# Top-k of the second mask in four pieces beside the first mask's scores, and mLSTM's q and k chunks set apart by v and the gates

## The chip, the cores and the metric

The kernel runs on one core of a Trainium2 chip. The engines named here are PE (TensorE, the matmul array; PEld is its weight load), DVE (VectorE), ACT (ScalarE), POOL (GpSimd) and SP (SyncE, which issues most DMAs). The metric is the device time of one execution in microseconds (us), as the median of several runs: 2522.85 us before, of 2522.05, 2522.85 and 2522.98.

## The reference

The program is a chain of blocks over 256 tokens of width 1024, all in fp32: two layers, each a mixer with three parallel branches and a SwiGLU feed-forward; then retention, a feed-forward, a short convolution, and a mixture of eight experts with a final norm. The change touches the mixer alone, which runs twice. Cut to what matters, it computes:

```python
def _layer(x, li, ...):
    z = rms(x, norm_mix_g) @ w_in
    (m_qk, m_v, m_o, m_if, s_q, s_ckv, i_q, i_k, i_w, d_q, d_k, d_v, g_pre) = split(z)
    m_qk = silu(causal_conv(m_qk, conv_w, conv_b))          # 4 taps, 1024 channels
    y_a = sigmoid(m_o) * rms(mlstm(mq, mk, m_v, m_if))      # 4 heads of 128
    y_b = dsa(rope(rms(s_q)), sk, sv, iq, ik, i_w)          # 8 heads of 64
    y_c = rms(diff_attn(rope(rms(d_q)), rope(rms(d_k)), d_v, lam))   # 4 heads, 2 x 64
    gates = sigmoid(g_pre + b_gate)                         # 3 x 1024
    merged = (gates[0] * (y_a @ w_branch[0]) + gates[1] * (y_b @ w_branch[1])
              + gates[2] * (y_c @ w_branch[2]))
    return x + merged @ w_out                               # then the feed-forward

def dsa(q, k, v, qi, ki, wi):        # for each query:
    score = sum over the 4 index heads of wi * relu(qi . ki), causal
    idx = top_k(score, 64)           # the 64 best keys of the 256
    return softmax(q . k[idx] / 8) @ v[idx]

def diff_attn(q, k, v, lam):
    p = softmax(causal(q . k / 8))   # for both halves of a head
    return (p[half 0] - lam * p[half 1]) @ v
```

## The kernel before

**Large matmuls.** An fp32 matmul is made of three: weights and activations are split into a high part and a rest, and high times high, rest times high and high times rest are added in PSUM (L224 to L226 in `gemm`; L256 to L258 in `gemmT`, which makes the transposed result). Weights come raw from memory by SP's queue into 4 buffers of 1 MB; for each 128x1024 piece ACT makes the high part (`hi`, L217) and DVE subtracts (`lo`, L218), each into one of 3 buffers. PE can work on such a chunk only as fast as both of them supply it, and runs at most 3 pieces behind. Results gather in 4 PSUM banks called `acc`; all small matmuls and transposes of the branches use 4 other banks called `mm`. A chunk of 512 output columns is 48 matmuls of 512 columns; its last matmul is followed by an evacuation on DVE or ACT that frees its two banks.

**Branches.** In `mixer` three generators hold the branches' small steps: `s` (the sparse attention, `dsa`), `f` (the differential attention, `diff`) and `m` (`mlstm`). Each `yield` ends a step. The string ORDER says in which order steps and chunks are written: a letter `s`, `f` or `m` takes the next step of that generator (nothing if it has ended); `dq`, `dk`, `dv`, `mv`, `o0`, `o1`, `q0` to `q3` (mLSTM's q and k, 256 columns each, by `gemmT`) and `g0` to `g5` (gates, 512 columns each) are chunks of the input projection; `b0`, `b1`, `c0`, `c1`, `a0`, `a1` are chunks of a branch's output projection, and the first of each drains that branch's generator. A scheduler then fixes each engine's queue in advance; the order in which things are written is their priority there. Every engine runs its own queue in order, so a matmul that waits holds all matmuls behind it.

**The sparse attention's steps.** After the scores of the index heads, the top-k of each of the two 128-query blocks (t = 0 and 1) is 8 rounds of MAX8 and MATCH_REPLACE8 on DVE (L588, L589), over 128 keys for t = 0 and 256 for t = 1; L592 to L594 make the mask from it. Then for each t four head pairs follow: scores on PE (L609), minus row maximum and mask on DVE (L547, `masked`), exponentials on ACT (L614), a transpose through PE (L539) and a copy by ACT (L541, `pT_of`), and the product with v on PE (L619).

**The differential attention's steps.** For the q and k rows: squares on ACT, sums, rope and norm on DVE (L460 to L462, L473, L481), the power for the norm on POOL (L192), and transposes on PE (L299). For each t, two head pairs: scores on PE (L675), `masked` (L547), exponentials with sums on ACT (L681), reciprocals (L686, L687), the scaling on ACT (L689) and the difference on DVE (L690), then a transpose (L539), its copy (L541) and the product with dv (L696). At a t's end ACT copies the row block out (`orow`, L700) and squares it four times (L470), POOL makes the power, DVE scales (L703); after both t, L274 transposes `orow`.

**Evacuations near the change.** A q chunk's result is scaled into `zp` (L740) and convolved (L746, three L748), with a tanh on ACT (L749) and L750. A gate chunk's is scaled and biased on DVE (L845; the bias row `bg` is loaded by SP for each chunk, L843) and goes through a tanh on ACT (L846). A line above 600 of the kernel before stands about 9 lines further down in the changed kernel: L539 and L547 are the same, L675 becomes L684, L696 becomes L705, L690 becomes L699, L845 becomes L854, L588 becomes L587.

Of the kernel before, what the change touches and what calls it, by code (L numbers as in the profile page):

```python
# [10 lines left out]
F32 = mybir.dt.float32  # L11
# [8 lines left out]
P = 128  # L20
# [6 lines left out]
NE = 8  # L27
BIG = 1e30
FILL = float(np.float32(1.5e38))
ORDER = ('dq s o0 s dv mg dk s o1 s s s s q0 s q1 s mh q2 q3 s s s s g3 s s g2 mv '  # L30
         'b0 f f f f f b1 f f f g4 f f g5 f m m m m g0 m m g1 c0 m c1 a0 a1')
WARM = 12
PRI1 = 200
NR1 = 3
# [15 lines left out]
TAKEN = float(np.float32(-3.3e38))  # L50
# [63 lines left out]
class Net:  # L114
# [305 lines left out]
    def mixer(self, li):  # L420
        nc, tc, I, sp = self.nc, self.tc, self.I, self.sp
        X = self.X
        with ExitStack() as es:
            zp_ = es.enter_context(tc.tile_pool(name="z4", bufs=18))
            mp = es.enter_context(tc.tile_pool(name="mix", bufs=1))
            tp = es.enter_context(tc.tile_pool(name="tmp", bufs=2))
            w2_ = es.enter_context(tc.tile_pool(name="w2", bufs=10))

            def z4(name, shape=(P, 2, 512), dt=F32):
                return zp_.tile(list(shape), dt, tag="z4", name=name)  # L430

            def w2(name, shape=(P, 512)):
                return w2_.tile(list(shape), F32, tag="w2", name=name)
# [92 lines left out]
            def qk_rows(src, which, dstT):  # L526
                rows = [w2("qkr") for _ in range(2)]
                for t in range(2):
                    normrope(src[:, t], which, rows[t], t)
                return lambda: self.plain_T(lambda t: rows[t], 4, dstT)  # L530

            def pT_of(prow, npair, t):

                pt = w2("pT")
                ps = self.mm_tile()
                k = 0
                for j in range(npair):
                    for s in range(t + 1):
                        nc.tensor.transpose(ps[:, k * P:(k + 1) * P], prow[:, j, s * P:(s + 1) * P], self.idt)  # L539
                        k += 1  # L540
                nc.scalar.copy(pt[:, :k * P], ps[:, :k * P])  # L541
                return pt[:, :k * P].rearrange("p (j s q) -> p j s q", j=npair, s=t + 1)

            def masked(dst, psv, m, nk, nm):

                for j in range(2):
                    nc.vector.tensor_tensor_reduce(dst[:, j, :nk], psv[:, j], m, -1.0, BIG, ALU.add, ALU.min, nm[:, j:j + 1])  # L547
# [3 lines left out]
            def new_yT():  # L551
                return z4("yTh", (P, 4, S), F32R), z4("yTl", (P, 4, S), F32R)

            def dsa():

                smask, scs = [None, None], [None, None]
                for t in range(2):
                    nk = P * (t + 1)
                    sc = tp.tile([P, 256], F32, tag="sc", name="sc")
                    nc.vector.memset(sc[:, :nk], 0.0)  # L560
                    for hp in range(2):
                        ps = self.mm_tile()
                        b = slice(hp * 64, hp * 64 + 64)
                        for j in range(2):
                            nc.tensor.matmul(ps[:, j * S:j * S + nk], iT[b, j, t * P:(t + 1) * P], iT[b, 2, :nk],
                                             start=True, stop=True)
                        rl = w2("rl", (P, 2, 256))
                        nc.scalar.activation(rl[:, :, :nk], ps.rearrange("p (j s) -> p j s", j=2)[:, :, :nk], AF.Relu)
                        for j in range(2):
                            h = j * 2 + hp  # L570
                            nc.vector.scalar_tensor_tensor(sc[:, :nk], rl[:, j, :nk], wi[:, t, h:h + 1], sc[:, :nk],
                                                           op0=ALU.mult, op1=ALU.add)
                    dsl = slice(t * P, (t + 1) * P)
                    nc.vector.tensor_tensor(sc[:, dsl], sc[:, dsl], self.cap, op=ALU.min)
                    scs[t] = sc
                sqT, skT = z4("sqT", (P, 4, S)), z4("skT", (P, 4, S))
                turn = qk_rows(zs, 0, sqT)
                yield
                turn()
                turn = qk_rows(skr, 1, skT)  # L580
                yield
                turn()
                for t in range(2):
                    nk = P * (t + 1)
                    sc, dsl = scs[t], slice(t * P, (t + 1) * P)
                    for i in range(8):
                        m8 = tp.tile([P, 8], F32, tag="m8", name="m8")  # L587
                        nc.vector.max(m8, sc[:, :nk])  # L588
                        nc.vector.match_replace(sc[:, :nk], m8, sc[:, :nk], TAKEN)  # L589
                    m = mp.tile([P, 256], BF16, name="smask", tag="smask%d" % t)  # L590
                    if t:
                        nc.vector.tensor_scalar(sc[:, :P], sc[:, :P], TAKEN, None, op0=ALU.is_equal)  # L592
                    nc.vector.scalar_tensor_tensor(sc[:, dsl], sc[:, dsl], TAKEN, self.lo01, op0=ALU.is_equal, op1=ALU.mult)
                    nc.vector.tensor_scalar(m[:, :nk], sc[:, :nk], -1.0, BIG, op0=ALU.add, op1=ALU.mult)  # L594
                    smask[t] = m
                    yield
                yb = z4("yb")
                for t in range(2):
                    nk = P * (t + 1)
                    po = self.mm_tile()  # L600
                    den = tp.tile([P, 8], F32, tag="den", name="den")
                    for q in range(4):
                        heads = [(q // 2) * 4 + (q % 2) + 2 * j for j in range(2)]
                        b = slice((q % 2) * 64, (q % 2) * 64 + 64)
                        ps = self.mm_tile()
                        psv = ps.rearrange("p (j s) -> p j s", j=2)[:, :, :nk]
                        for j in range(2):
                            hp = heads[j] // 2
                            nc.tensor.matmul(psv[:, j], sqT[b, hp, t * P:(t + 1) * P], skT[b, hp, :nk], start=True, stop=True)  # L609
                        nm = tp.tile([P, 2], F32, tag="nm", name="nm")  # L610
                        pr = w2("pr", (P, 2, 256))
                        masked(pr, psv, smask[t][:, :nk], nk, nm)
                        for j in range(2):
                            nc.scalar.activation(pr[:, j, :nk], pr[:, j, :nk], AF.Exp, bias=nm[:, j:j + 1], scale=-1.0,  # L614
                                                 accum_out=den[:, heads[j]:heads[j] + 1])
                        pt = pT_of(pr, 2, t)
                        for j, h in enumerate(heads):
                            for s in range(t + 1):
                                nc.tensor.matmul(po[:, h * 64:(h + 1) * 64], pt[:, j, s], sv[:, s, h * 64:(h + 1) * 64],  # L619
                                                 start=s == 0, stop=s == t)  # L620
                        if q < 3:
                            yield
                    rd = tp.tile([P, 8], F32, tag="rd", name="rd")
                    nc.vector.reciprocal(rd, den)
                    nc.vector.tensor_mul(yb[:, t].rearrange("p (h d) -> p h d", d=64), po.rearrange("p (h d) -> p h d", d=64),
                                         rd[:, :, None].to_broadcast([P, 8, 64]))
                    yield
                yT["b"] = new_yT()
                self.split_T(lambda t: yb[:, t], 4, *yT["b"])


            dq, dk, dv = {}, {}, {}
# [218 lines left out]
            def branch(key, b, c0):  # L851
                def ev(t, c0, n, ps):
# [6 lines left out]

            mqk_chunk = lambda c0: (lambda: self.gemmT(xs, 8, W, [c0], ev_qk))  # L860
            gens = {"s": dsa(), "f": diff(), "m": mlstm()}
            work = {"dq": chunk(3148, 512, ev_into(dq, "dq")), "dk": chunk(3660, 512, ev_into(dk, "dk")),
                    "dv": chunk(4172, 512, ev_into(dv, "dv")), "mv": chunk(1024, 512, ev_mv),
# [5 lines left out]
            for key, gen, b in (("b", "s", 1), ("c", "f", 2), ("a", "m", 0)):  # L869
                for hf in range(2):  # L870
# [4 lines left out]
                    work["%s%d" % (key, hf)] = br  # L875
            for w in ORDER.split():
                if w in gens:
# [479 lines left out]
```

## Time and profile before

| what | value |
|---|---|
| median of 3 runs | 2522.85 us |
| profiled execution | 2522.33 us |
| its span | 2520.2 us |
| its granted PE clock, mean | 0.994 of full |
| the two mixers | about 5 to 270 us and 480 to 750 us of the span |

All times of rows are microseconds from the start of the span of that one execution, unless a column says otherwise. The time outside the span is 2.1 us. An engine's busy time counts what overlaps once; the 512-column matmuls of the chunks are pipelined, so that one lasts 0.39 us in its row while the next starts 0.23 us after it. The clock column is what the throttle granted to PE: 1.00 is 2.4 GHz, 0.50 is 1.2 GHz.

### The profile page before, as it was taken

What the parts mean: (1) busy time and instruction counts of PE and PEld (TensorE: products, weight loads), DVE (VectorE), ACT (ScalarE), POOL (GpSimd) and SP (SyncE); (2) the same over time, 40 slices, a digit from 0 to 9 for tenths busy, and PEclk for the clock granted to TensorE, in tenths of its full rate; (3) what the DMA queues carried; (4) which work ended last, traced back from release to release, by engine and by line L of the source; (5) the groups of instructions that cost most, each with busy time, mean ns of one, the idle gap of its engine ahead of it and who ended that gap; (6) DMA issues with size and microseconds to landing.
All of it is one profiled execution on the core that took longest, in us unless ns stands there. A gap on an engine that the chain in (4) does not pass through costs nothing. (4 is left out here: it accounts for less than half of the span.)

```text
span 2520.2 us, 32185 instructions
## 1 busy us (share of the span) xinstructions
PE 2483.6 (99%) x12113; PEld 2050.6 (81%) x12113; DVE 1888.0 (75%) x2533; ACT 1569.0 (62%) x2127; POOL 71.3 (3%) x47
## 2 busy tenths in 40 slices
PE   9999999999999999999999999999999999999997
PEld 8877888888788888878888988888887888788886
DVE  6987755578785457445555869999988898889887
ACT  6556544565655445545444448878777777777776
POOL 0110000020100000000000000000000000000000
PEclk9999999999999999999999999999999999999999
DMA  6544555464545556546555847999999999999993
GB/s 236 174 156 151 175 184 180 159 197 138 171 158 177 191 172 204 170 161 238 187 191 189 291 160 264 349 355 349 361 360 340 347 349 368 345 347 348 374 349 143
DMA packets 325139, 614.78 MB, mean 244 GB/s; under 512 B 10984, under 2 KB 44016, under 8 KB 324848
## 3 DMA queue, kind: packets, MB, share of 16 engines
q1 hardware_dynamic: 324192, 610.97, 70.3%
q8 instruction: 97, 1.59, 0.2%
q0 software_dynamic: 352, 1.06, 0.1%
q10 hardware_dynamic: 432, 0.62, 0.1%
q14 instruction: 66, 0.54, 0.1%
HBM read 611.55 MB, written 1.06 MB: 243 GB/s over the span
## 5 line engine op out<-in xcount | busy, mean ns | idle before, releaser
L218 DVE TENSOR_TENSOR lo<-raw,hi 128x1024 fp32r<-128x1024 f32 (+1 forms) x1156 | 1376.9, 1215 | 545.6 <-ACT hi L217 528.6
L217 ACT CAST hi<-raw 128x1024 fp32r<-128x1024 f32 (+1 forms) x1156 | 1188.3, 1047 | 703.3 <-PE acc L226 353.5
L225 PE MATMUL mm<-lo,gh 128*128 128x512 f32 x896 | 353.2, 394 | 1.1
L224 PE MATMUL mm<-hi,gh 128*128 128x512 f32 x896 | 349.4, 390 | 2.6 <-ACT ST L1163 2.5
L226 PE MATMUL mm<-hi,gl 128*128 128x512 f32 x896 | 348.9, 390 | 0.0
L226 PE MATMUL acc<-hi,hTl 128*128 128x512 f32 x736 | 290.4, 395 | 0.0
L225 PE MATMUL acc<-lo,hTh 128*128 128x512 f32 x736 | 289.6, 394 | 0.0
L224 PE MATMUL acc<-hi,hTh 128*128 128x512 f32 x736 | 289.0, 393 | 0.0
L224 PE MATMUL acc<-hi,xTh 128*128 128x512 f32 (+3 forms) x672 | 254.8, 382 | 2.6 <-ACT hi L217 2.2
L225 PE MATMUL acc<-lo,xTh 128*128 128x512 f32 (+3 forms) x672 | 252.7, 377 | 1.3 <-DVE lo L218 1.2
L226 PE MATMUL acc<-hi,xTl 128*128 128x512 f32 (+3 forms) x672 | 250.8, 375 | 0.0
L224 PE MATMUL mm<-hi,xTh 128*128 128x512 f32 (+1 forms) x608 | 230.3, 379 | 0.0
L226 PE MATMUL mm<-hi,xTl 128*128 128x512 f32 (+1 forms) x608 | 229.8, 378 | 0.0
L225 PE MATMUL mm<-lo,xTh 128*128 128x512 f32 (+1 forms) x608 | 229.8, 378 | 0.0
L225 PEld LDWEIGHTS mm<-lo,gh 128*128 128x128 f32 x896 | 168.1, 188 | 50.9 <-DVE lo L218 17.1
L224 PEld LDWEIGHTS mm<-hi,gh 128*128 128x128 f32 x896 | 168.2, 188 | 38.7 <-ACT ST L1163 2.9
L226 PEld LDWEIGHTS mm<-hi,gl 128*128 128x128 f32 x896 | 168.2, 188 | 33.8
L224 PEld LDWEIGHTS acc<-hi,hTh 128*128 128x128 f32 x736 | 138.3, 188 | 28.1
L225 PEld LDWEIGHTS acc<-lo,hTh 128*128 128x128 f32 x736 | 138.3, 188 | 27.5
L226 PEld LDWEIGHTS acc<-hi,hTl 128*128 128x128 f32 x736 | 138.4, 188 | 26.6
L224 PEld LDWEIGHTS acc<-hi,xTh 128*128 128x128 f32 x672 | 127.6, 191 | 26.9 <-ACT hi L217 2.6
L225 PEld LDWEIGHTS acc<-lo,xTh 128*128 128x128 f32 x672 | 127.6, 190 | 24.6 <-DVE lo L218 3.6
(364 smaller groups left out, 3032.4 us busy)
## 6 DMA issues: line engine op xcount, KB each, us to landing
raw<-in_moe_w_up SPq DMA_DIRECT2D x112, 1024.0 KB, 6.5
raw<-in_moe_w_down SPq DMA_DIRECT2D x112, 1024.0 KB, 6.5
raw<-in_moe_w_gate SPq DMA_DIRECT2D x112, 1024.0 KB, 6.8
raw<-in_w_in SPq DMA_DIRECT2D x52, 1024.0 KB, 5.1
raw<-in_w_gate_up SPq DMA_DIRECT2D x40, 1024.0 KB, 5.1
raw<-in_ret_w_in SPq DMA_DIRECT2D x24, 1024.0 KB, 5.0
raw<-in_w_down SPq DMA_DIRECT2D x20, 1024.0 KB, 5.0
raw<-in_ffn_w_gate SPq DMA_DIRECT2D x14, 1024.0 KB, 5.1
```

The source lines that it names most:

```text
L217: nc.scalar.copy(hi[:, :m], r)
L218: nc.vector.tensor_sub(lo[:, :m], r, hi[:, :m].bitcast(F32))
L224: mm(ps, xh, wh, start=first, stop=False)
L225: mm(ps, xh, wl, start=False, stop=False)
L226: mm(ps, xl, wh, start=False, stop=last)
```

## The change

The second mask's eight rounds are no longer a step of their own. Two rounds are written behind each of the four head-pair steps of t = 0, and the mask behind the last; so `s` has one step fewer before the scores. In ORDER the chunks q0 to q3 are put apart: mv, g3 and g2 move from behind the sparse attention to between them, q3 moves to directly before b0, and the steps `s` are spread anew. At the end one `m` step (mLSTM) goes ahead of the `f` that stood behind g5 (before: `g5 f m m m m g0`, now: `g5 m f m m m g0`).

```diff
@@ -27,8 +27,8 @@
 NE = 8
 BIG = 1e30
 FILL = float(np.float32(1.5e38))
-ORDER = ('dq s o0 s dv mg dk s o1 s s s s q0 s q1 s mh q2 q3 s s s s g3 s s g2 mv '
-         'b0 f f f f f b1 f f f g4 f f g5 f m m m m g0 m m g1 c0 m c1 a0 a1')
+ORDER = ('dq s o0 s dv mg dk s o1 s q0 s s mv s q1 s mh g3 s q2 s g2 s s q3 '
+         'b0 f f f f f b1 f f f g4 f f g5 m f m m m g0 m m g1 c0 m c1 a0 a1')
 WARM = 12
 PRI1 = 200
 NR1 = 3
@@ -580,20 +580,25 @@
                 turn = qk_rows(skr, 1, skT)
                 yield
                 turn()
-                for t in range(2):
+
+                def rounds(t, n):
+                    for i in range(n):
+                        m8 = tp.tile([P, 8], F32, tag="m8", name="m8")
+                        nc.vector.max(m8, scs[t][:, :P * (t + 1)])
+                        nc.vector.match_replace(scs[t][:, :P * (t + 1)], m8, scs[t][:, :P * (t + 1)], TAKEN)
+
+                def chosen(t):
                     nk = P * (t + 1)
                     sc, dsl = scs[t], slice(t * P, (t + 1) * P)
-                    for i in range(8):
-                        m8 = tp.tile([P, 8], F32, tag="m8", name="m8")
-                        nc.vector.max(m8, sc[:, :nk])
-                        nc.vector.match_replace(sc[:, :nk], m8, sc[:, :nk], TAKEN)
                     m = mp.tile([P, 256], BF16, name="smask", tag="smask%d" % t)
                     if t:
                         nc.vector.tensor_scalar(sc[:, :P], sc[:, :P], TAKEN, None, op0=ALU.is_equal)
                     nc.vector.scalar_tensor_tensor(sc[:, dsl], sc[:, dsl], TAKEN, self.lo01, op0=ALU.is_equal, op1=ALU.mult)
                     nc.vector.tensor_scalar(m[:, :nk], sc[:, :nk], -1.0, BIG, op0=ALU.add, op1=ALU.mult)
                     smask[t] = m
-                    yield
+                rounds(0, 8)
+                chosen(0)
+                yield
                 yb = z4("yb")
                 for t in range(2):
                     nk = P * (t + 1)
@@ -618,6 +623,10 @@
                             for s in range(t + 1):
                                 nc.tensor.matmul(po[:, h * 64:(h + 1) * 64], pt[:, j, s], sv[:, s, h * 64:(h + 1) * 64],
                                                  start=s == 0, stop=s == t)
+                        if t == 0:
+                            rounds(1, 2)
+                            if q == 3:
+                                chosen(1)
                         if q < 3:
                             yield
                     rd = tp.tile([P, 8], F32, tag="rd", name="rd")
```

How the queues change is shown at three places of the first layer; the second layer has the same pieces. First PE's queue in the middle of the differential attention, in the kernel before: L539 transposes the probabilities (`ar`) of t = 0's second head pair, L696 is their product with dv, L675 (256 columns) the scores of t = 1's first pair, and `acc<-` rows are matmuls of a gate chunk.

```order
L224 MATMUL acc<-hi,xTh 128x512
L539 MATMUL mm<-ct,ar 128x128 x2
L675 MATMUL mm<-dkT,dqT 128x256 x3
L696 MATMUL mm<-dv,pT 128x128 x2
L675 MATMUL mm<-dkT,dqT 128x256
L225 MATMUL acc<-lo,xTh 128x512
L226 MATMUL acc<-hi,xTl 128x512
L224 MATMUL acc<-hi,xTh 128x512
L225 MATMUL acc<-lo,xTh 128x512
```

Behind these rows 34 more matmuls of gate chunks follow before the next small step. In the changed kernel the same steps (L684 and L705 are L675 and L696 of before) stand so on PE; the row after the last shown is the first matmul of g0:

```order
L539 MATMUL mm<-ct,ar 128x128 x2
L705 MATMUL mm<-dv,pT 128x128 x2
L684 MATMUL mm<-dkT,dqT 128x128 x4
L539 MATMUL mm<-ct,ar 128x128
L684 MATMUL mm<-dkT,dqT 128x256
L539 MATMUL mm<-ct,ar 128x128
L684 MATMUL mm<-dkT,dqT 128x256 x2
L705 MATMUL mm<-dv,pT 128x128 x2
L684 MATMUL mm<-dkT,dqT 128x256
L539 MATMUL mm<-ct,ar 128x128 x4
L705 MATMUL mm<-dv,pT 128x128 x4
L684 MATMUL mm<-dkT,dqT 128x256 x4
```

Here L539 and L705 first finish t = 0's first pair; then come that block's second pair (L684 x4, two L539, L705) and t = 1's first pair with the scores of its second, and no chunk matmul stands among these 12 rows. Between the scores of a pair and its transposes there stand 19 chunk matmuls for t = 0's first pair, none for its second, none for t = 1's first, and 25 for the last; before there were 19, 36 and 31 for the last three.

The second place is DVE's queue where the first mask is made (`smask`) and the first scores of t = 0 arrive (L547 writes `pr`); MAX and MATCH_REPLACE over 128x256 are rounds of the second mask. Before:

```order
L588 MAX m_1009<-sc 128x8
L593 SCALAR_TENSOR_TENSOR sc<-sc,ct 128x128
L589 MATCH_REPLACE sc<-m_1009,sc 128x256
L594 TENSOR_SCALAR smask<-sc 128x128
L218 TENSOR_TENSOR lo<-raw,hi 128x1024
L588 MAX m_1012<-sc 128x8
L547 ISA pr,nm<-mm,smask 128x128
L547 ISA nm 128x1
L589 MATCH_REPLACE sc<-m_1012,sc 128x256
L547 ISA pr,nm<-mm,smask 128x128
L547 ISA nm 128x1
```

And in the changed kernel, where L587 and L588 are the rounds and L596 and L597 the mask:

```order
L587 MAX m_1028<-sc 128x8
L596 SCALAR_TENSOR_TENSOR sc<-sc,ct 128x128
L588 MATCH_REPLACE sc<-m_1028,sc 128x256
L597 TENSOR_SCALAR smask<-sc 128x128
L218 TENSOR_TENSOR lo<-raw,hi 128x1024
L547 ISA pr,nm<-mm,smask 128x128
L547 ISA nm 128x1
L547 ISA pr,nm<-mm,smask 128x128
L547 ISA nm 128x1
L587 MAX m_1031<-sc 128x8
L588 MATCH_REPLACE sc<-m_1031,sc 128x256
```

One MAX of the second mask stands behind the first two L547 instead of ahead of them, and the rounds follow in pairs behind each step.

The third place is DVE's queue from the rows that make the sparse attention's result ready for b0 (`yTl`, L281) on, where the differential attention's q rows are normed and roped (L460 to L462). Before:

```order
L281 TENSOR_TENSOR yTl<-mm,yTh 128x512 x2
L845 SCALAR_TENSOR_TENSOR gate<-acc,xrs,bg 128x512
L218 TENSOR_TENSOR lo<-raw,hi 128x1024
L845 SCALAR_TENSOR_TENSOR gate<-acc,xrs,bg 128x512
L190 TENSOR_SCALAR rsqv<-ss 128x8
L460 TENSOR_TENSOR rp<-dq,tabs 128x512
L218 TENSOR_TENSOR lo<-raw,hi 128x1024
L845 SCALAR_TENSOR_TENSOR gate<-acc,xrs,bg 128x512 x2
L218 TENSOR_TENSOR lo<-raw,hi 128x1024
L461 TENSOR_TENSOR qkr<-dq,tabs 128x512
L460 TENSOR_TENSOR rp<-dq,tabs 128x512
```

In the changed kernel (L749, L755, L757 and L759 are q3's evacuation and convolution, L864 the merge of branch b, L854 would be a gate's):

```order
L281 TENSOR_TENSOR yTl<-mm,yTh 128x512 x2
L749 TENSOR_TENSOR zp<-acc,bc 128x256 x2
L218 TENSOR_TENSOR lo<-raw,hi 128x1024
L755 TENSOR_SCALAR cv<-zp,gc 128x256 x2
L757 SCALAR_TENSOR_TENSOR cv<-zp,gc,cv 128x256 x3
L218 TENSOR_TENSOR lo<-raw,hi 128x1024
L757 SCALAR_TENSOR_TENSOR cv<-zp,gc,cv 128x256 x2
L864 SCALAR_TENSOR_TENSOR gate<-gate,acc 128x512
L218 TENSOR_TENSOR lo<-raw,hi 128x1024
L759 SCALAR_TENSOR_TENSOR mqk<-zp,cv 128x256
L757 SCALAR_TENSOR_TENSOR cv<-zp,gc,cv 128x256
```

The rows for a gate's evacuation are gone from here, and q3's convolution and branch b's merge stand there instead; the first row of the differential attention's norm (L190) follows two rows below the last one shown.

## Rows read from the trace of the kernel before

**Rows 1.** Page, busy time of each engine.

```profile
PE 2483.6 (99%) x12113; PEld 2050.6 (81%) x12113; DVE 1888.0 (75%) x2533; ACT 1569.0 (62%) x2127; POOL 71.3 (3%) x47
```

**Rows 2.** Waits of PE: line, releaser, us in total, times, longest.

```profile
PE mm L539 <- ACT pr L614: 3.4, 3, 2.1
...
PE mm L274 <- DVE orow L703: 1.8, 2, 0.9
PE mm L299 <- DVE qkr L481: 1.4, 2, 0.7
...
PE mm L539 <- DVE ar L690: 0.6, 2, 0.3
```

**Rows 3.** Timeline of PE (start, duration): second head pair of t = 0.

```profile
194.99 0.72 PE L675 MATMUL mm<-dkT,dqT 64*128 64x128 f32 x8
195.64 0.50 PE L224 MATMUL acc<-hi,xTh 128*128 128x512 f32 x1
...
200.33 0.50 PE L539 MATMUL mm<-ct,ar 128*128 128x128 f32 x2
200.76 1.13 PE L675 MATMUL mm<-dkT,dqT 64*128 64x256 f32 x6
```

**Rows 4.** Timeline of ACT and DVE in that stretch and behind it.

```profile
197.63 1.04 ACT L217 CAST hi<-raw 128x1024 fp32r<-128x1024 f32 x1
197.75 0.18 DVE L686 RECIPROCAL dden<-dden 128x4 f32<-128x4 f32 x1 [1.09 <-ACT dp L681]
...
198.57 0.69 ACT L689 ACTIVATE dp<-dp,dden 128x128 f32<-128x128 f32 x2
...
199.84 0.61 DVE L690 SCALAR_TENSOR_TENSOR ar<-dp,dden 128x128 f32<-128x128 f32 x2
...
201.02 0.36 ACT L541 COPY pT<-mm 128x256 f32<-128x256 f32 x1
202.56 0.58 ACT L700 COPY orow<-mm 128x512 f32<-128x512 f32 x1 [1.18 <-PE mm L696]
203.18 0.31 ACT L470 ACTIVATE sq<-orow 128x128 f32<-128x128 f32 x1
...
204.37 0.49 ACT L681 ACTIVATE dp<-dp,nm 128x256 f32<-128x256 f32 x1
```

**Rows 5.** Windows: stretch, us, busy of each engine (x), PEclk, DMA, GB/s.

```profile
99.60:103.00 3.40, 3.40 (x19) 3.40 (x18) 3.11 (x9) 1.30 (x4) 0.00 (x0) 0.50 0.63 214
...
228.00:230.00 2.00, 1.09 (x8) 0.70 (x7) 1.34 (x3) 1.17 (x2) 0.63 (x1) 1.00 0.00 0
```

**Rows 6.** Timeline of DVE and POOL: norm and rope of the differential attention.

```profile
172.98 4.28 POOL L192 TENSOR_TENSOR rsq<-rsqv,nhalf 128x8 f32<-128x8 f32 x1 [1.06 <-DVE rsqv L190]
...
179.21 1.22 DVE L218 TENSOR_TENSOR lo<-raw,hi 128x1024 fp32r<-128x1024 f32 x1
180.34 0.16 DVE L190 TENSOR_SCALAR rsqv<-ss 128x8 f32<-128x8 f32 x1
180.42 0.68 DVE L460 TENSOR_TENSOR rp<-dk,tabs 128x512 f32<-128x512 f32 x1
181.02 0.68 DVE L461 TENSOR_TENSOR qkr<-dk,tabs 128x512 f32<-128x512 f32 x1
...
183.23 0.69 DVE L481 TENSOR_TENSOR qkr<-qkr,rsq 128x512 f32<-128x512 f32 x1 [0.80 <-POOL rsq L192]
...
204.74 1.01 POOL L192 TENSOR_TENSOR rsq<-rsqv,nhalf 128x4 f32<-128x4 f32 x1 [21.55 <-DVE rsqv L190]
```

**Rows 7.** Groups of DVE by line: min/median/max ns, first and last start.

```profile
L748 DVE SCALAR_TENSOR_TENSOR cv<-zp,gc,cv x48: 462/476/482, 108.5 to 617.3; 128x256 f32<-128x256 f32 x48
...
L845 DVE SCALAR_TENSOR_TENSOR gate<-acc,xrs,bg x24: 730/743/751, 156.5 to 723.5; 128x512 f32<-128x512 f32 x24
```

**Rows 8.** Timeline of DVE: second mask's round ahead of the first scores.

```profile
98.05 0.42 DVE L588 MAX8 m<-sc 128x8 f32<-128x256 f32 x1
98.39 0.27 DVE L547 CUSTOM_DVE_ANT_0 pr<-mm,smask 128x128 f32<-128x128 f32 x1
```

## The prediction

> **What bounds the kernel now.** I read the page's busy times first: PE is busy 2483.6 us of the 2520.2 us span [rows 1], so only 36.6 us of it are without a matmul, and DVE (75%) and ACT (62%) have room on the average. The kernel is bound by PE, and the change neither adds nor takes a matmul. It can win only some of the 36.6 us, but it can lose any amount, by opening holes in PE's queue. Second, PE's waits [rows 2]: those in the two mixers that the change touches are small (L539 on the sparse attention's `pr` 3.4 us, L274 on `orow` 1.8, L299 on `qkr` 1.4, L539 on `ar` 0.6, all over both layers). Third, the timeline around the differential attention, to see why they are small: a head pair's chain (scores, mask, exponentials, difference, transposes) takes from 194.99 to 200.33, 5.34 us, and 19 chunk matmuls run meanwhile [rows 3]; they fill 4.69 us, 0.25 us each with the change-over. The cover hides the chain, so its length costs only the 0.3 us per layer at `ar`. Last, the order of PE's instructions in the changed kernel: this cover is what moved.
>
> **The dense stretch (both layers).** ORDER now spends g2, g3 and mv on the sparse attention, and g4 and g5 are used up when the differential attention's first pair has its scores transposed. The twelve rows shown above follow each other on PE with no chunk matmul, and since PE's queue runs in order, g0's matmuls behind them can't start early, even with their weights there. I walk through it, in us from the first pair's scores, whose cover of 19 matmuls stands as before:
> - 5.3: the first pair's transposes, as before. Their product L705 needs ACT's copy, which now stands behind two casts in ACT's queue; before, the 1.06 us of score matmuls between transposes and product covered it [rows 3]. A copy 0.36 and part of the casts (1.04 each) [rows 4], which began while the matmuls still ran: 0.9 idle.
> - The second pair's scores, 0.65 as at 194.99 to 195.64, and then its chain bare. In the trace it took 5.34, but a cast (1.04 at 197.63) and a `lo` subtraction stood in it on ACT and DVE. Without them, the reciprocals from 197.75 take 0.5, then one half of L689 (0.35) and L690, and the transposes follow L690's start by 0.5 [rows 4, 3]: about 199.1. That makes 4.1, of which the scores are 0.65: 3.5 idle. The scores of t = 1's first pair run between its two transposes and after.
> - The product waits for its copy (0.36 and the hand-over): 0.5 idle.
> - t = 1's first pair. ACT copies `orow` (0.62 with the hand-over), squares it four times (203.18 to 204.37: 1.19), and only then makes the four exponentials (4 x 0.49 = 1.98) [rows 4]; reciprocals 0.5, L698 0.45 for 256 columns, L699 0.45 follow. 5.2, against 0.3 of scores on PE with some hand-overs: 5.1 idle.
> - The product of t = 1's first pair waits for a copy of 512 columns: 0.75 idle.
> In sum 10.75 idle per layer, against about 0.5 in the same steps before (0.3 at `ar` [rows 2], some tenths at the products): +10.3 per layer, **+20.6**. Nothing gives it back: DVE and ACT fill three pieces of weights ahead while PE idles, but afterwards PE works off its chunks at its own speed. Bounds per layer: 5.1 if only the long wait stands and the others hide in hand-overs, 13 if two more copies and casts get in the way; over both layers +10 to +26. I take the walk, since each link has a row.
>
> **The clock behind it.** After the 2.1 us wait at L539 [rows 2] PE ran the 3.4 us from 99.60 at a granted clock of 0.50 (1.2 GHz); a wait of 0.9 us at 229 left it at 1.00 [rows 5]. The stretch has waits of 3.5 and 5.1 us in each layer. If 3.4 us behind each stretch, and the small matmuls in it, go at half speed, it is 1.7 + 0.3 per layer: **+4.0**, from 0 to +6.8 (twice that behind each stretch). The Trainium skill ("TensorE: Matmul & The Clock Gate", section "HAM oscillation — how this bites in real kernels") says that waits between bursts of matmuls put the array back to half rate and that the next burst starts there; the row at 99.60 agrees. By it the sum is as I give it, without it 4.0 less.
>
> **The differential attention's rows.** q3 is now directly ahead of b0, so its convolution (12 instructions of 0.40 to 0.48 [rows 7]) and tanh lie on DVE and ACT where q and k are normed and roped; two gate evacuations (0.74 each) left that place. From b0's first evacuations to the last transposes DVE has by the changed order 9 `lo` at 1.13 (179.21 to 180.34 [rows 6]), 12 of the convolution at 0.40 apart, 4 of branch b's merge and 19 rows of 512 columns at 0.60 apart (180.42 to 181.02 [rows 6]): 10.2 + 4.8 + 13.8 = 28.8, with the small ones 29.1. PE has 120 chunk matmuls at 0.23 and small ones there: 29.0. Before there was slack, and the wait at L299 was 0.7 a layer [rows 2]. With DVE as full as PE, the powers on POOL between L190 and L481 (2.9 us from 180.34 to 183.23, of which 0.80 was idle [rows 6]) show. I take 1.5 more per layer: **+3.0**, from -1.8 (both waits and the hand-overs go) to +7 (each power's wait shows). A power took 4.28 us beside a busy DVE and 1.01 beside an idle one [rows 6]. The Trainium skill ("GPSIMD Engine Reference", section "8. Key points") says that POOL shares its way to SBUF with DVE; the two rows agree. In the dense stretch the power of `orow` isn't on the path that I walked, but behind it; at 4.28 there it would add up to 3.3 per layer, and the sum would be about 2554.
>
> **What is won.** The transposes of `orow` had 11 chunk matmuls behind t = 1's last product and waited 0.9 per layer [rows 2]; now 29 stand there: **-1.8** (0 to -1.8). In the sparse attention one MAX stood ahead of the first two L547 (98.05 to 98.39: 0.34 [rows 8]) and now stands behind them; with the later waits at `pr` (one of 0.4 a layer) that makes **-1.4** (0 to -5: all of L539's 3.4 and the half clock behind it). The 16 instructions of the second mask's rounds are the same, and run beside scores which DVE finishes early enough.
>
> **The rest.** The last head pairs of the sparse attention lie beside g2, whose two evacuations on DVE (0.74 each [rows 7]) and tanh on ACT get between softmax and transposes: **+1.0** (0 to +1.5). The `m` step written ahead of `f` changes DVE's and ACT's queue by a few short rows that PE doesn't wait for: 0, up to +0.5 if the decay weights come ahead of a mask. The bias rows come by SP as before.
>
> **Sum.** 20.6 + 4.0 + 3.0 - 1.8 - 1.4 + 1.0 = +25.4. On the profiled execution's 2522.33 this gives 2547.7; the median of the runs before is 0.5 above that execution, so 2548.
>
> **Rivals.**
> - B, not slower: PE's stretch is no stretch. Each chain finishes while PE does the step in front of it, because ACT and DVE, without casts to make, run ahead of PE. Then the stretch adds at most 1.6 per layer (the copies), L299's waits go (-1.8) and the gains stand (-1.8, -1.4): 2522.85 + 3.2 - 5.0 = 2521 at most, 2518 with no copy to wait for. It decides if a bare chain is below about 1.5 us. Against it: the chain's links lie one behind the other in rows 3 and 4 and add up to over 4 us.
> - C, heavier: the clock stays at 0.50 through the stretch and longer, and norm and rope come late by the whole power wait. 2548 + 2.8 (clock to its bound) + 4 (to its bound of 7) + 3 (casts in the chains) = 2558. For it: two holes of over 3 us so close together; against: PE was back at full clock 3.4 us after the wait at 97 [rows 5].
> - D, lighter: only the wait behind `orow` and the squares stands (5.1 per layer), and the clock doesn't fall: 2522.85 + 10.2 + 3.0 - 3.2 + 1.0 = 2534. For it: ACT and DVE have little else to do in the stretch, so hand-overs may be shorter.
>
> **How the numbers follow.** My forecast has 0.74, with its own range from 2537 to 2558; C 0.13, D 0.08, B 0.05. The range from 2533 to 2560 takes in D and C and leaves out B and what lies beyond the bounds. About 0.2% (5 us) is what a measurement of this kernel can tell from no change. B is split between faster and no change; a D that is lighter still adds nothing there: faster 0.02, same 0.03, slower 0.95.
>
> **What would show it right or wrong.** The profile's waits of PE should have new rows for L539 on `ar` (L699) of about 8 to 9 us per layer, in two waits of 3 to 4 and about 5 us, and L705 on the copy (L541) of about 2 per layer. A window of the stretch should show PE busy under half of some 15 us, and the clock at 0.50 behind it. L274 on `orow` should be gone, L299 on `qkr` should have grown to 3 to 5 in all, and L539 on `pr` should be around 2 to 3. Wrong would be: chunk matmuls in the stretch, or chains below 2 us there.

## The result, and the profile after

The changed kernel takes 2554.45 us (median of 4 runs, 2552.35 to 2557.0), against 2522.45 for the kernel before on the same chip: a ratio of 1.0131, with a 95% interval from 1.0119 to 1.0143. It is slower by 32 us; 2548 was predicted, with a range from 2533 to 2560. The profiled execution of the changed kernel has a span of 2551.5 us, 31.3 more than before.

The page's busy times of the changed kernel [rows 1]:

```profile
PE 2495.0 (98%) x12113; PEld 2054.7 (81%) x12113; DVE 1891.4 (74%) x2533; ACT 1569.0 (61%) x2127; POOL 73.0 (3%) x47
```

The same 12113 matmuls keep PE busy for 11.4 us more, and PE is idle for 56.5 us instead of 36.6: the loss is 19.9 us of waiting and 11.4 us of slower matmuls (one profile of each kernel). The waits of PE in the changed kernel (line, releaser, us in total, times, longest) answer to [rows 2]:

```profile
PE mm L539 <- DVE ar L699: 16.0, 4, 4.5
PE mm L539 <- ACT pr L619: 3.2, 3, 1.8
PE mm L299 <- DVE qkr L481: 3.2, 4, 1.4
PE mm L705 <- ACT pT L541: 3.1, 4, 0.9
...
PE acc L224 <- DVE gate L864: 1.8, 2, 0.9
...
PE mm L274 <- DVE ya L839: 0.7, 2, 0.4
```

L539 on `ar` had 0.6 us before and L705's line none. They now have 19.1 us in the dense stretch, 9.5 per layer. PE's timeline (start, duration) shows the stretch of the first layer, in place of [rows 3]:

```profile
209.38 0.50 PE L539 MATMUL mm<-ct,ar 128*128 128x128 f32 x2
210.75 0.71 PE L705 MATMUL mm<-dv,pT 128*128 128x128 f32 x4 [0.86 <-ACT pT L541]
211.39 0.72 PE L684 MATMUL mm<-dkT,dqT 64*128 64x128 f32 x8
215.62 0.45 PE L539 MATMUL mm<-ct,ar 128*128 128x128 f32 x1 [3.51 <-DVE ar L699]
216.00 1.22 PE L684 MATMUL mm<-dkT,dqT 64*128 64x256 f32 x2
...
219.86 1.22 PE L684 MATMUL mm<-dkT,dqT 64*128 64x256 f32 x2
225.57 1.09 PE L539 MATMUL mm<-ct,ar 128*128 128x128 f32 x4 [4.49 <-DVE ar L699]
227.33 2.08 PE L705 MATMUL mm<-dv,pT 128*128 128x128 f32 x8 [0.68 <-ACT pT L541]
229.34 2.09 PE L684 MATMUL mm<-dkT,dqT 64*128 64x256 f32 x8
231.35 0.74 PE L224 MATMUL acc<-hi,xTh 128*128 128x512 f32 x1
```

No chunk matmul lies between 209.38 and 231.35, and the two bare chains stand as waits of 3.51 and 4.49 us. The last rows show the other part of the loss: eight scores of 256 columns last 2.09 us here, against 1.14 before (at 214.21). The windows of the stretch (us, busy of PE, PEld, DVE, ACT, POOL, then PEclk, DMA, GB/s) say why:

```profile
209.50:212.40 2.90, 1.75 (x14) 1.19 (x13) 2.54 (x6) 1.20 (x2) 0.00 (x0) 1.00 0.16 13
212.40:216.00 3.60, 0.38 (x2) 0.18 (x2) 1.72 (x12) 2.34 (x10) 0.00 (x0) 0.84 1.07 341
216.00:219.00 3.00, 3.00 (x9) 1.48 (x9) 0.19 (x1) 0.37 (x1) 0.00 (x0) 0.50 0.17 20
...
221.00:226.00 5.00, 0.51 (x3) 0.41 (x3) 3.09 (x11) 3.73 (x16) 1.01 (x1) 0.50 0.00 0
...
229.00:230.80 1.80, 1.80 (x10) 1.32 (x9) 0.00 (x0) 0.00 (x0) 0.00 (x0) 0.50 0.00 0
...
232.00:233.00 1.00, 1.00 (x6) 0.83 (x5) 0.92 (x6) 1.00 (x5) 0.00 (x0) 1.00 0.00 0
```

The granted clock falls in the first wait, 0.8 us before its end (0.85 in a window from 214.5 to 215.0, 0.50 in the next), and stays at 0.50 (1.2 GHz) until g0's matmuls begin; at 232 it is back at 1.00. In the second layer the stretch is the same, but g0's matmuls, which begin at 721.37 there, run for some 2 us at half clock too:

```profile
721.40:723.40 2.00, 2.00 (x7) 1.61 (x6) 1.47 (x8) 1.47 (x6) 0.00 (x0) 0.50 0.00 0
```

PE is busy for some 10 us between 212.4 and 230.8 almost wholly at 0.50, so about 5 us per layer are lost on the small matmuls, 10 of the 11.4; g0's first matmuls of the second layer lose about 1 more.

The other waits that are new lie just ahead, where q and k are normed. PE, DVE and POOL there, against [rows 6]:

```profile
192.62 4.89 POOL L192 TENSOR_TENSOR rsq<-rsqv,nhalf 128x8 f32<-128x8 f32 x1 [3.39 <-DVE rsqv L190]
...
197.55 0.69 DVE L481 TENSOR_TENSOR qkr<-qkr,rsq 128x512 f32<-128x512 f32 x1 [1.53 <-POOL rsq L192]
...
198.39 0.41 PE L299 MATMUL mm<-ct,qkr 128*128 128x128 f32 x2 [1.35 <-DVE qkr L481]
...
200.16 0.50 PE L224 MATMUL acc<-hi,xTh 128*128 128x512 f32 x1 [0.90 <-DVE gate L864]
```

The power on POOL ends at 197.5; DVE waits 1.53 us for it and PE 1.35 for DVE, then another 0.90 for branch b's merge, which stands behind the norm in DVE's queue.

### The profile page after: what moved, and what is told of

Its sections match the earlier page's. It is cut to its first block, busy times and chain, and to the rows that moved or that the text cites. A ratio compares the mean times of both kernels' runs of the same rounds, so it can differ in the third digit from the quotient of the medians.

```text
span 2551.5 us, 32171 instructions
## 1 busy us (share of the span) xinstructions
PE 2495.0 (98%) x12113; PEld 2054.7 (81%) x12113; DVE 1891.4 (74%) x2533; ACT 1569.0 (61%) x2127; POOL 73.0 (3%) x47
```

## The experiments

The theory: ORDER leaves the differential attention's chains without chunk matmuls beside them, and PE pays the bare chains and the half clock that they bring. The rivals: the split rounds cost; the chunks' new places cost by what they put on DVE and ACT; the waiting alone, without the clock, is the loss. Each ratio is to the kernel before in runs on the same chip; these took 2520.2 to 2520.8 us, about 2 less than beside the change above, so a window that was expected in us lies about 2 too high for them.

**The new ORDER alone** (order_only). The second mask's rounds are one step again:

```diff
-ORDER = ('dq s o0 s dv mg dk s o1 s s s s q0 s q1 s mh q2 q3 s s s s g3 s s g2 mv '
-         'b0 f f f f f b1 f f f g4 f f g5 f m m m m g0 m m g1 c0 m c1 a0 a1')
+ORDER = ('dq s o0 s dv mg dk s o1 s s q0 s s mv s q1 s mh g3 s q2 s g2 s s q3 '
+         'b0 f f f f f b1 f f f g4 f f g5 m f m m m g0 m m g1 c0 m c1 a0 a1')
```

> The new ORDER with the old sparse attention: the second mask's eight rounds are one step again (one more s directly behind o1's). Theory (the dense stretch without chunk matmuls comes from ORDER): PE's queue has the same 12 rows but for one or two matmuls, so 2550 us, between 2545 and 2557, with about 8 us per layer of waits at L539 on ar. Rival (the rounds that now run beside the first mask's scores delay masks and scores): without the split most of the loss is gone, 2522 to 2530.

2558.36 us, ratio 1.015 (1.0135 to 1.0166): the whole loss and a little more, just above the theory's window. Its waits of PE:

```profile
PE mm L539 <- DVE ar L690: 15.6, 5, 4.5
PE mm L299 <- DVE qkr L481: 3.7, 2, 2.3
PE acc L224 <- DVE gate L855: 3.5, 2, 2.6
```

The stretch is there without the split. The split may even be worth about 0.2% in this order (1.015 against 1.0131, but the two intervals overlap): without it the waits at the norm and at branch b's merge are longer (7.2 us against 5.0), and in the first layer the granted clock fell beside them, to 0.79 in the window from 190 to 205, against 1.00 in the change. Why the first layer has these waits longer wasn't followed further.

**The split alone** (topk_only): the changed kernel's rounds, ORDER as before with one `s` fewer.

```diff
-... dk s o1 s q0 s s mv s q1 s mh g3 s q2 s g2 s s q3 b0 ... g5 m f m m m g0 ...
+... dk s o1 s s s q0 s q1 s mh q2 q3 s s s s g3 s s g2 mv b0 ... g5 f m m m m g0 ...
```

> The split rounds with the old ORDER (one s fewer behind o1, as there is one step fewer). PE's queue around the differential attention is that of the kernel before. Theory: the stretch is not there, 2518 to 2523, the gain coming from L539's waits on the sparse attention's probabilities (3.4 us before). Rival (the rounds delay masks and scores): 2530 to 2550.

2521.16 us, ratio 1.0001 (0.9992 to 1.001): nothing. The first rival falls. The expected gain isn't there either:

```profile
PE mm L539 <- ACT pr L619: 3.3, 3, 1.8
...
PE mm L274 <- DVE orow L712: 1.8, 2, 0.9
```

L539's waits on the probabilities are 3.3 us as against 3.4 [rows 2].

**The chain earlier** (early_f). Two `f` steps go ahead of q3, all chunks stay where the change put them:

```diff
-... q2 s g2 s s q3 b0 f f f f f b1 ...
+... q2 s g2 f s f s q3 b0 f f f b1 ...
```

> The changed kernel with the first two f steps (norm and rope of the differential attention's q and k rows) written ahead of q3 instead of behind b0; q3, v and the gates stay where the change put them. PE's queue then has 43 and 1 to 36 chunk matmuls between scores and transposes again. Theory (the loss is that the chain of the differential attention starts too late for the chunks that could cover it): no wait of over 1 us at L539 on ar, 2518 to 2528. Rival (the chunks' new places cost by themselves, by DVE and ACT work of q3, g2 and g3 beside other steps): above 2535.

2530.06 us, ratio 1.0038 (1.0025 to 1.0051), just outside the theory's window. No wait at `ar` is left among PE's waits, and none for branch b's merge; with them and their clock about seven tenths of the loss went (1.0131 against 1.0038). The rest is in the page and the waits:

```profile
PE 2488.5 (98%) x12113; PEld 2053.4 (81%) x12113; DVE 1891.2 (75%) x2533; ACT 1568.9 (62%) x2127; POOL 66.2 (3%) x47
```

```profile
PE mm L299 <- DVE qkr L481: 4.3, 2, 2.2
```

Two waits of 2.2 us at L299 and 4.9 us more of busy PE than before [rows 1]: norm and rope now press on the sparse attention's end, and behind these waits the granted clock falls again (0.54 in the window from 178.80 to 182.30, 0.51 from 653.30 to 660.10).

**The clock held up** (keep_clock). Matmuls that nobody reads fill the two long waits:

```diff
+KEEP = {(0, 1): 12, (1, 0): 18, (1, 1): 0}
...
                 ps = self.mm_tile()
+                for _ in range(keep):
+                    nc.tensor.matmul(ps, KX[:, 0, 0:P], KX[:, 0:2], start=True, stop=True)
```

> The changed kernel with matmuls added whose result nobody reads: 12 of 512 columns ahead of the second pair's transposes of t = 0 and 18 ahead of those of t = 1's first pair, 2.7 and 4.1 us, both shorter than the waits of 3.5 and 4.5 us there. Theory (a third of the loss is the small matmuls at a granted clock of 0.50): the clock stays at 1.00 through the stretch, its small matmuls take 5 us instead of 10.5 per layer, and the time falls by about 10 to 2544 (2541 to 2548), although work is added. Rival (the loss is waiting alone): 2553 to 2558.

2547.11 us, ratio 1.0105 (1.0089 to 1.012): 0.26% or 6.6 us less than the change, with 60 matmuls more. The two intervals just touch, so the size of the gain is rough; what happened to the clock is in the trace. Windows and timeline of its stretch:

```profile
217.30:222.00 4.70, 4.70 (x24) 3.34 (x24) 1.72 (x9) 3.52 (x15) 1.00 (x1) 1.00 0.03 7
222.00:227.00 5.00, 3.71 (x22) 2.54 (x20) 1.97 (x5) 2.18 (x7) 0.01 (x1) 1.00 0.00 0
```

```profile
219.34 4.38 PE L539 MATMUL mm<-xTh 128*128 128x512 f32 x18
224.34 0.83 PE L543 MATMUL mm<-ct,ar 128*128 128x128 f32 x4 [0.62 <-DVE ar L703]
225.85 1.16 PE L709 MATMUL mm<-dv,pT 128*128 128x128 f32 x8 [0.68 <-ACT pT L545]
226.94 1.14 PE L688 MATMUL mm<-dkT,dqT 64*128 64x256 f32 x8
229.25 0.50 PE L225 MATMUL acc<-hi,xTh 128*128 128x512 f32 x1 [1.17 <-DVE gate L858]
```

The clock stays at 1.00 through the stretch, and the eight scores last 1.14 us instead of 2.09. The clock's part is shown. It didn't give the full 10 us: g0 now waits 1.17 us per layer for a gate's evacuation on DVE, which is a new wait, and in the first layer the clock was low ahead of the stretch (0.53 in the window from 200.8 to 204.2).

**One link shorter** (squares_later). The four squares, the power and the scaling of `orow` move behind the product of t = 1's first pair:

```diff
                         if hp == 0:
+                            if t:
+                                fin(0)
                             yield
                     nc.scalar.copy(orow[:, t], po)
-                    r = head_rms(orow[:, t], 4, 128, "or")
-                    ov = orow[:, t].rearrange("p (h d) -> p h d", d=128)
-                    nc.vector.tensor_mul(ov, ov, r[:, :, None].to_broadcast([P, 4, 128]))
+                    if t:
+                        fin(1)
```

> The changed kernel with the four squares of orow (t = 0), its power and its scaling written behind the product of t = 1's first pair instead of ahead of that pair's exponentials; PE's queue stays as it is. Theory (the wait of 4.5 us at L539 in the stretch is the sum of a chain of links, and the squares, 1.19 us on ACT, are one of them): that wait falls to between 2.7 and 3.4 per layer, the other waits of the stretch stay, and the time falls by 2 to 4 us against the changed kernel, to 2551. Rival (the wait has another end, such as DVE or a transfer): the wait stays at 4.5.

2554.77 us, ratio 1.0136 (1.012 to 1.0151): no change in time, where 2 to 4 us less were expected. PE's waits and the second of the long ones:

```profile
PE mm L539 <- DVE ar L704: 13.7, 4, 3.5
...
PE acc L224 <- DVE gate L860: 2.3, 2, 1.2
...
223.63 1.09 PE L539 MATMUL mm<-ct,ar 128*128 128x128 f32 x4 [3.33 <-DVE ar L704]
```

The wait fell from 4.49 to 3.33, by 1.16, close to the squares' 1.19, so they are a link of that chain. (The power and the scaling moved with them, but in the change the scaling ended on DVE at 223.87, when the last exponential on ACT had just ended at 223.83, and held nothing up.) The gain went into a wait of 1.2 per layer at a gate's evacuation, which now stands behind the power and the scaling on DVE.

**q3 away, g2 ahead of b0** (g2_last).

```diff
-... q1 s mh g3 s q2 s g2 s s q3 b0 ...
+... q1 s mh g3 s q2 s q3 s s g2 b0 ...
```

> The changed kernel with q3 written ahead of the last three s steps and g2 directly ahead of b0. The stretch without chunk matmuls is the same in PE's queue but for one matmul. Theory (q3's convolution on DVE where q and k are normed and roped costs the waits at L299 and at the merge of branch b, 5.0 us in all after against 1.4 before): these two fall to 2 or less, the waits at L539 on ar stay at 15 to 16, and the time is 2550 (2546 to 2553). Rival (norm and rope are late whatever stands there, because v and the gates no longer lie beside them): both waits stay at 4 to 5 and the time at 2553 to 2557.

2535.31 us, ratio 1.006 (1.0045 to 1.0076). That is outside both windows. The expectation read PE's queue wrongly: 18 chunk matmuls stand there between the second pair's scores and its transposes, so one chain is bare and not two.

```profile
PE mm L539 <- DVE ar L699: 10.6, 4, 5.0
...
PE mm L299 <- DVE qkr L481: 1.4, 2, 0.7
...
PE mm L705 <- ACT pT L541: 1.4, 2, 0.7
```

L299's waits are those of before [rows 2], and the wait for branch b's merge is gone. That fits q3's convolution as their cause, but g2's matmuls also cover the norm now; the run can't part the two.

**The old tail** (old_tail): `g5 f m m m m g0`.

> The changed kernel with the old tail of ORDER (f ahead of the four m steps). Theory (the place of the m step doesn't touch the stretch): waits at L539 on ar unchanged at 16, the wait of L274 on orow back with 1.8, so 2554 to 2558. Rival (the m step ahead of f makes the chain late): under 2550, with shorter waits at ar.

2552.99 us, ratio 1.0129 (1.0113 to 1.0144), 16.0 us at `ar` and 1.8 at `orow` again: the place of the `m` step leaves the stretch as it is. It moves the waits at `orow`, but no time to speak of (1.0129 against 1.0131); the waits of 0.7 at `ya` that the change has are not there.

**All cover back** (mv_last). The split, q chunks apart and the new tail, with g3, g2 and mv ahead of b0:

```diff
-... q0 s s mv s q1 s mh g3 s q2 s g2 s s q3 b0 ...
+... q0 s s q1 s mh s q2 s q3 s g3 s s g2 mv b0 ...
```

> The split rounds, the q chunks kept apart by s steps, and the new tail, but g3, g2 and mv back directly ahead of b0, so that PE's queue has 19 to 36 chunk matmuls between scores and transposes. Theory (the loss is the missing cover alone): 2517 to 2523, with no wait over 0.5 at ar and none at orow. Rival (q chunks apart cost by themselves): 2527 or more.

2520.34 us, ratio 1.0001 (0.9992 to 1.001). The waits at `ar` are 0.4 us in all, and none is left at `orow`. q's chunks may stand apart; v and the gates in their old place, with q3 ahead of them, take the whole loss away.

**Bias rows in their own pool** (bias_pool). The order is that of the change:

```diff
+W2B = 9
...
-            w2_ = es.enter_context(tc.tile_pool(name="w2", bufs=10))
+            w2_ = es.enter_context(tc.tile_pool(name="w2", bufs=W2B))
+            bg_ = es.enter_context(tc.tile_pool(name="bgp", bufs=2))
...
-                    bg[0] = w2("bg")
+                    bg[0] = bg_.tile([P, 512], F32, tag="bg", name="bg")
```

> The changed kernel with the gates' bias rows in a pool of their own of 2 buffers (w2 keeps 9 of 10), where before they took turns in w2 with the differential attention's probabilities. In PE's queue 33 chunk matmuls now stand between the scores of t = 1's first pair and its transposes; only the second pair of t = 0 is still bare. Theory (g0's matmuls stand behind the stretch since a gate's bias row, and with it the evacuation that frees a PSUM bank, comes only when the differential attention gives a w2 buffer back): one bare chain of 3.5 us and less time at half clock are left, 2537 (2532 to 2543), with 7 to 8 us of waits at L539 on ar. Rival (the chain is late for chunks whatever their buffers): 2550 or more.

2546.78 us, ratio 1.01 (1.0084 to 1.0115): better than the change by 0.3%, but between the theory's window and the rival's. PE's waits, one of its rows and, at the end, its busy time and two windows of the stretch:

```profile
PE mm L541 <- DVE ar L701: 7.8, 4, 3.5
PE mm L817 <- DVE hrow L833: 3.7, 2, 1.9
...
255.53 0.67 PE L817 MATMUL mm<-mqk 128*128 128x256 f32 x2 [1.86 <-DVE hrow L833]
```

```profile
PE 2495.7 (98%) x12113; PEld 2055.8 (81%) x12113; DVE 1891.4 (74%) x2533; ACT 1569.2 (62%) x2127; POOL 69.6 (3%) x47
...
212.00:218.00 6.00, 3.26 (x9) 1.54 (x10) 1.98 (x8) 2.31 (x10) 0.00 (x0) 0.52 0.15 58
218.00:224.00 6.00, 6.00 (x18) 4.38 (x19) 3.34 (x12) 4.66 (x19) 1.01 (x1) 0.62 0.00 1
```

The mechanism holds: with bias rows of their own g0's matmuls come early enough to cover t = 1's first pair, and `ar` falls to 7.8 us. But g0's and g1's matmuls are then missing where mLSTM's last steps needed them, and L817 waits 3.7 us in a place that had no wait. Cover was moved, not made. And the clock cost as much as in the change: PE is busy 12.1 us more than before [rows 1]. It fell in the one bare wait of 3.51 us that is left, g0's chunk matmuls then ran at half speed from 220.13 to 222.7, and the clock is low once more behind the wait at L817 (0.55 from 257.00 to 260.40). So the expectation of less time paid at half clock was wrong.

**The same pool with all cover back** (bias_pool_mv_last).

> The same bias pool in the order that had mv, g3 and g2 back ahead of b0. Theory: that order has cover everywhere already, so the pool has nothing to give: 2517 to 2523. Rival (the gates' evacuations waited for bias rows there too): 2515 or less.

2518.58 us, ratio 0.9989 (0.998 to 0.9998): the fastest of all, by 0.11% faster than the kernel before, within the expected window and its interval just clear of 1. What gave these 2 us wasn't followed.

## Why the prediction was right, and where its sizes were off

The direction, the place and the mechanism were right, and the time lies inside the range. By steps, as forecast and as the two profiles have it:

| step | forecast | measured |
|---|---|---|
| dense stretch, waits | +20.6 | 19.1 - 0.6 = +18.5 |
| clock | +4.0 | +11.4 of busy PE |
| norm and rope | +3.0 | L299 +1.8, merge of b +1.8 = +3.6 |
| `orow` | -1.8 | -1.8, but +0.7 at `ya` |
| sparse attention, g2 beside it | -0.4 | -0.2 at `pr` |

**The stretch.** The walk gave 0.9, 3.5, 0.5, 5.1 and 0.75 us of idle time; the trace has 0.86, 3.51, nothing, 4.49 and 0.68. The copy of 0.5 is hidden by the scores of t = 1's first pair, which run at half clock before it. The chain behind `orow`'s copy took 5.6 us (219.97 to 225.57), a little more than walked, but the wait is shorter than 5.1 because the last scores behind the product took 1.15 us of PE at half clock and not 0.3. That a chain's links add up is shown by squares_later, and that ORDER alone makes the stretch by order_only, early_f and mv_last.

**The clock is the term that was mis-sized**, at 4.0 for 11.4 us. The forecast put 3.4 us of chunk matmuls behind each stretch at half speed and gave the small ones 0.3. Most of it came the other way: the small matmuls ran at 0.50 from 215.6 to 231, about 5 us lost per layer, and the chunk matmuls behind them were at full clock after 0.6 us in the first layer and some 2 us in the second. keep_clock shows that the price is real, and that about 6.6 us of it can be had back without any cover. The row that I sized it by, 3.4 us at 0.50 from 99.60 [rows 5], had a single wait with chunk matmuls behind it; this stretch had two waits with only small ones between. The rival C named this (the clock stays at 0.50 through the stretch), but as an extra of 2.8 us. The Trainium skill ("TensorE: Matmul & The Clock Gate", section "HAM oscillation — how this bites in real kernels") says that a wait between bursts puts PE back to half rate and that the next burst starts there; the windows agree, with 0.50 from 216.00 to 219.00 behind the wait of 3.51 us.

**The power of `orow`.** In the stretch, at 222.14 with DVE idle around it, it took 1.01 us and delayed nothing, so the sum of 2554 that stood on 4.28 us there came near the result for another reason. The 4.28 and 1.01 [rows 6] that the prediction set side by side are of different sizes, 128x8 and 128x4. Of the 128x8 powers in the change, with DVE busy all the while, one took 4.70 us (at 59.26) and one 1.95 (at 187.28); the four-column power took 1.31 beside a DVE that was busy throughout (265.88). That a busy DVE alone makes the power four times as long is not shown.

**Norm and rope** came out at 3.6 for 3.0, half of it as foreseen through the power and L481 (4.89 us on POOL at 192.62), half at branch b's merge, which I hadn't named: it stands behind the norm on DVE and holds PSUM banks. **`orow`.** The waits went as forecast, with 29 chunk matmuls in place of 11; old_tail shows that the `m` step's place does it, and that the time doesn't follow. **The split's gain** of 1.4 wasn't there: topk_only puts it at nothing. In the first layer the longest wait fell from 2.1 to 1.8 us with the MAX gone from ahead of L547, but the three waits together went only from 3.4 to 3.3: in the second layer the next transposes wait longer instead.

**Rival D** forecast 2534 if only the wait behind `orow` and its squares stands; g2_last, where one chain alone is bare, measured 2535.31. That is in part chance: D counts 3.0 for norm and rope and nothing for the clock, while g2_last has L299 as before and 3.3 us more of busy PE (2486.9). **Rival B**, chains that finish under the step in front, falls with the 3.51 and 4.49 us.

## What to carry to other kernels

In a kernel that its matmuls bound, a chunk of independent matmuls is cover, and there is only so much: before moving one, look in the bounding engine's queue at what stands between the first and last step of each long chain through the other engines, at the place that it leaves. A bare chain costs nearly its whole length (4.49 of 5.6 us here), and on PE the small matmuls between two such waits cost nearly double besides (2.09 us for 1.14). Cover put behind such a wait doesn't save that: in bias_pool the chunk matmuls paid it instead. Which chunk can be cover is also set by shared buffers: here a bias row of a gate had to wait for a buffer of the chain that it was to cover.

## What the runs showed of the hardware beyond what was expected

PE's granted clock fell while it waited (0.84 in the window from 212.4 to 216, with 0.38 us of 3.6 busy). Small matmuls that then kept PE busy without a gap from 215.62 to 221.08 did not bring it back before the next wait came. Behind the second wait it was at 1.00 by 232 in the first layer, 0.6 us into the dense 512-column matmuls, and by 723.5 in the second, some 2 us into them; what brings it back no run here shows. Matmuls that nobody reads, put into waits of 3.5 and 4.5 us, kept it at 1.00 and nearly halved the small matmuls' time (2.09 to 1.14 us for eight).
